# A hybrid decoder layer: the state-space products of eight heads in one block, attention by two heads, norm sums in float32r, decay products later

## The chip, the cores and the metric

One NeuronCore of a Trainium2 chip runs the kernel; the other cores are idle. The metric is device time in microseconds of one execution. Five engines work side by side, each on its own list of instructions: TensorE (matrix products and transposes, results into PSUM), VectorE, ScalarE, GpSimd (POOL) and SyncE, whose queue loads the weights. PSUM has eight banks of 128 x 512 float32; this kernel gives three to the large products (tag `pj`) and five to everything else (tag `bg`).

## The reference, cut to what matters

One layer, 256 tokens of width 1024, all float32, batch 1:

```python
h = h + 0.5 * rmsnorm(swiglu(rmsnorm(h, ...), w_gate, w_up, w_down), ...)      # width 2816
u = rmsnorm(h, mix_pre_g)
z, xbc, dt_raw, q, k, v, gate_logits = split(u @ w_in)
y_ssd = ssd_branch(z, xbc, dt_raw, ...)           # 32 heads of 64, 4 groups of 8 heads, state 128
y_att = diff_attn_branch(q, k, v, ...)            # 8 heads, two score maps each, values 128 wide
merged = gates[:, :, 0] * y_ssd + gates[:, :, 1] * y_att
h = h + rmsnorm(merged @ w_out, mix_post_g)
h = h + 0.5 * rmsnorm(swiglu(...), ...)           # a second feed-forward layer
```

The state-space branch: a causal convolution over four tokens and SiLU on x, B and C; dt = softplus(dt_raw + bias); for every head, y[t] = sum over s <= t of (C[t]·B[s]) exp(acum[t] - acum[s]) dt[s] x[s], with acum the running sum of dt times a negative number of the head; then + D x, times SiLU(z), and a norm over each group's 512 channels. The attention: for each head, softmax(map 1) - lam softmax(map 2), both causal with a linear penalty on distance, times v, and a norm over each head's 128 outputs.

## The kernel before, in words

**Products.** Weights come in chunks of 1 MB. Each chunk is split into a high part rounded to float32r (ScalarE, `L168`) and the rest (VectorE, `L169`), and three products replace one: high x high, high x low and low x high (`mm_t` `L195`, `mm_nat` `L208`). A chunk used by `mm_t` is 48 products with 256 moving columns, one used by `mm_nat` 24 products with 512. Small products (scores, decays, the state-space products, the norm sums) are in plain float32, which the trace shows as two records each; transposes show as one.

**Buffers.** Tag `k4` holds 29 tiles of 4 KB a partition (weight halves and long-lived activations), `k3` three tiles of 3 KB (the decay matrices `E` of two heads, later the scores of an attention head), `k2` seven of 2 KB. `take()` splits weights three chunks ahead of their use.

**Stages.** Feed-forward 1; v; B and C (four chunks, `L762`); x (eight); z (eight); q and k (eight); gates (eight chunks of 512 columns); the state-space branch's output product `pws` (eight); the attention branch's output product `pwd` (four); `w_out`; feed-forward 2. Before the B and C chunks stand dt's product, softplus as a polynomial on VectorE (`L693` to `L731`) and the decay products `pac` with the triangle of ones (`L733` to `L738`), whose result goes to DRAM (`acd`) and comes back spread over all partitions (`acb`).

**The background.** The state-space work, the norms and the attention are generators which stop at priced places (`yield 1.8`). After each half of the large products the code calls `back.run(us)`, which adds `us` to an account and lets the generators issue steps until the account is used up; a `BREAK` ends the run early. The prices: 3.15 a chunk in the z and q/k stages, 1.35 per 12 products in the gate stage, 1.55 in `pws` and in the first half of `pwd`. Behind the first chunk of `pwd`, `attended()` issues all that is left. In the state-space work, each pair of heads makes E and then at once its products `py` (`L813` to `L817`), where each head fills one half of the 128 columns of the array; the VectorE update of xs (`L819`) follows. Attention is a pipeline by single heads: scores of head n, transposes of head n-1, combination of head n, values of head n-1, norm of a pair every second head, transposes of the pair's result one head later.

**Order.** Up to the gate stage the order on TensorE is made by a planner from program order and its own clock of when operands are ready; from `L1063` on TensorE follows program order exactly. ScalarE and VectorE are ordered by the planner from the v stage on.

Of the kernel before, what the change touches and what calls it, by code (L numbers as in the profile page):

```python
# [14 lines left out]
F32 = mybir.dt.float32  # L15
# [9 lines left out]
P = 128  # L25
T = 256
# [4 lines left out]
H_SSD = 32  # L31
H_ATT = 8
NEG = -1e30
K4_BUFS = 29
K3_BUFS = 3
K2_BUFS = 7
RAW_BUFS = 3
AHEAD = 3
# [11 lines left out]
def tile_hybrid_layer(ctx: ExitStack, tc: tile.TileContext, x, ffn1_pre_g, ffn1_w_gate, ffn1_w_up,  # L50
# [33 lines left out]
    def bg(shape, name):  # L84
        return ps.tile(shape, F32, tag="bg", name=name, bufs=5)
# [137 lines left out]
    def act_table(name):  # L223
        f = nc.scalar.preload_act_table_set(name)
        for prev in act_since:
            tc.add_manual_dep(f.ins, prev, order, reason="activation table")
        act_since.clear()
        act_fence[0] = f.ins.name

    def act(*args, **kw):  # L230
        a = nc.scalar.activation(*args, **kw)
# [39 lines left out]
    nc.gpsimd.memset(nhalf, -0.5)  # L271
    ones = const.tile([P, P], F32, name="ones")
    nc.gpsimd.memset(ones, 1.0)

    pw = bg([P, P], "warm")

# [416 lines left out]
    ptd = bg([P, 2, H_SSD], "ptd")  # L693
    for b in range(2):
        nc.tensor.transpose(ptd[:, b, :], dtT[:, b * P:(b + 1) * P], ident[:H_SSD, :H_SSD])
    shp = [P, 2, H_SSD]
    dx = const.tile(shp, F32, name="dx")
    nc.vector.tensor_tensor(dx, ptd, dtb.unsqueeze(1).to_broadcast(shp), ALU.add)
    e = const.tile(shp, F32, name="dte")
    w2 = const.tile(shp, F32, name="dtw2")  # L700
    pol = const.tile(shp, F32, name="dtp")
    dt = const.tile(shp, F32, name="dt")

    act_table(EXP_LN)

    lp = const.tile([P, 2, 64], F32, name="lp")
    lvv = lv.rearrange("p (a b) d -> p a b d", b=2)
    tc.keep_in_program_order(nc.vector.tensor_tensor(lp, lvv[:, :, 0, :], lvv[:, :, 1, :], ALU.mult))
    ld = const.tile([P, 2], F32, name="ld")
    nc.vector.tensor_reduce(ld, lp, AX.X, ALU.add)  # L710
    act(ld, ld, AF.Exp)
    nlam = const.tile([P, 1], F32, name="nlam")
    nc.vector.tensor_sub(nlam, ld[:, 1:2], ld[:, 0:1])
    nc.vector.tensor_scalar(nlam, nlam, -0.2, None, ALU.add)
    act(aexp, aexp, AF.Exp)

    nc.scalar.activation(e, dx, AF.Abs)
    act(e, e, AF.Exp, scale=-1.0)
    act_table(SILU)
    nc.vector.tensor_scalar(w2, e, 2.0, None, ALU.add)  # L720
    nc.vector.reciprocal(w2, w2)
    nc.vector.tensor_tensor(e, e, w2, ALU.mult)
    nc.vector.tensor_tensor(w2, e, e, ALU.mult)
    nc.vector.tensor_scalar(pol, w2, 1.0 / 17, None, ALU.mult)
    for n in (15, 13, 11, 9, 7, 5, 3):
        nc.vector.scalar_tensor_tensor(pol, pol, 1.0 / n, w2, ALU.add, ALU.mult)
    nc.vector.scalar_tensor_tensor(pol, pol, 1.0, e, ALU.add, ALU.mult)
    nc.vector.tensor_scalar(dx, dx, 0.0, None, ALU.max)
    nc.vector.scalar_tensor_tensor(dt, pol, 2.0, dx, ALU.mult, ALU.add)
    av = const.tile(shp, F32, name="av")  # L730
    nc.vector.scalar_tensor_tensor(av, dt, -1.0, aexp.unsqueeze(1).to_broadcast(shp), ALU.mult, ALU.mult)  # L731

    pac = bg([P, 512], "pac")  # L733
    for b in range(2):
        nc.tensor.matmul(pac[:H_SSD, b * P:(b + 1) * P], av[:, b, :], tri, start=True, stop=True)
    nc.tensor.matmul(pac[:, 256:288], tri, av[:, 0, :], start=True, stop=True)
    nc.tensor.matmul(pac[:, 288:320], tri, av[:, 1, :], start=True, stop=True)
    nc.tensor.matmul(pac[:, 320:352], after_m, av[:, 0, :], start=True, stop=True)  # L738
    acT = k2([H_SSD, T], "acT")
    nc.scalar.activation(acT, pac[:H_SSD, :T], AF.Copy, scale=-1.0)  # L740
    acs = const.tile([P, 3, H_SSD], F32, name="acs")
    nc.scalar.copy(acs, pac[:, 256:352].rearrange("p (a h) -> p a h", a=3))
    acd = dram.tile([H_SSD, T], F32, name="acd")
    nc.gpsimd.dma_start(acd, acT)


    cw = lambda k, c: cols_b[:, k * 24 + c:k * 24 + c + 1]

# [35 lines left out]
    def ssd_work(groups):  # L784
        for g in groups:
            X = k4([P, 2, 512], f"X{g}")
            for b in range(2):
                px = bg([P, 4, P], f"px{g}{b}")
                for c in range(4):
                    nc.tensor.transpose(px[:, c, :], xs[g][:, c, b * P:(b + 1) * P], ident)  # L790
                nc.vector.tensor_tensor(
                    X[:, b, :].rearrange("p (e q) -> p e q", q=64),
                    px.rearrange("p c (e q) -> p (c e) q", q=64),
                    dt[:, b, g * 8:(g + 1) * 8].unsqueeze(2).to_broadcast([P, 8, 64]), ALU.mult)
                yield 0.6
            for hf in range(2):
                acb = k4([P, 4, T], f"acb{g}{hf}")
                r0 = g * 8 + hf * 4
                nc.gpsimd.dma_start(acb, acd[r0:r0 + 4, :].partition_broadcast(P))
                py = bg([P, 2, T], f"py{g}{hf}")  # L800
                for pr in range(2):
                    E = k3([P, 2, 3 * P], f"E{g}{hf}{pr}")
                    for i in range(2):
                        hd = r0 + pr * 2 + i
                        lh = pr * 2 + i
                        act(E[:, i, :P], acb[:, lh, P:], AF.Relu, bias=acs[:, 1, hd:hd + 1])
                        nc.vector.tensor_scalar(E[:, i, P:T], acb[:, lh, :P], acs[:, 0, hd:hd + 1], 0.0,
                                                ALU.add, ALU.max)
                        act(E[:, i, T:], acb[:, lh, P:], AF.Exp, bias=acs[:, 2, hd:hd + 1], scale=-1.0)
                    act(E[:, :, :T], E[:, :, :T], AF.Exp, scale=-1.0)  # L810
                    nc.vector.tensor_tensor(E, E, cbm[g].unsqueeze(1).to_broadcast([P, 2, 3 * P]), ALU.mult)
                    c = hf * 2 + pr
                    for i in range(2):  # L813
                        xc = slice(c * P + i * 64, c * P + (i + 1) * 64)
                        os = slice(i * 64, (i + 1) * 64)
                        nc.tensor.matmul(py[os, pr, :], X[:, 0, xc], E[:, i, P:], start=True, stop=False)
                        nc.tensor.matmul(py[os, pr, P:], X[:, 1, xc], E[:, i, :P], start=False, stop=True)  # L817
                    dc = 96 + g * 4 + c
                    nc.vector.scalar_tensor_tensor(xs[g][:, c, :], xs[g][:, c, :], cols_b[:, dc:dc + 1],  # L819
                                                   py[:, pr, :], ALU.mult, ALU.add)  # L820
                    yield 1.8

    def ssd_norm(groups):

        def one(g):
# [3 lines left out]
            yield 1.2  # L829
            nc.vector.tensor_tensor(sq[:, 0:2, :], sq[:, 0:2, :], sq[:, 2:4, :], ALU.add)  # L830
            nc.vector.tensor_tensor(sq[:, 0, :], sq[:, 0, :], sq[:, 1, :], ALU.add)
            yield 1.1
            yield BREAK
            pn = bg([P, T], f"pn{g}")
            nc.tensor.matmul(pn, ones, sq[:, 0, :], start=True, stop=True)
# [133 lines left out]
    def att_work():  # L969


        pairs = [Pair(hp) for hp in range(4)]
        heads = [Head(hd, pairs[hd // 2]) for hd in range(H_ATT)]
        for n in range(H_ATT + 2):
            if n < H_ATT:
                heads[n].scores()
                yield 2.3
            if 0 < n <= H_ATT:
                heads[n - 1].turn()
                if n % 2 == 1 and opens:  # L980
                    opens.pop()()
            if n < H_ATT:
                heads[n].combine()
                yield 1.3
            yield BREAK
            if 0 < n <= H_ATT:
                heads[n - 1].values()
                if n % 2 == 0:
                    pairs[n // 2 - 1].norm()
                    yield 1.8  # L990
                    if n == H_ATT:
                        yield BREAK
            if n >= 3 and n % 2 == 1:
                pairs[(n - 3) // 2].turn()
                yield 0.8

    class Background:

# [190 lines left out]
```

## Time and profile before

| what | value |
|---|---|
| median of 3 runs | 746.06 us (745.94 to 746.64) |
| profiled execution | 746.09 us, of it 744.4 us span |
| TensorE busy | 734.7 us, 99% |
| VectorE, ScalarE, POOL busy | 67%, 56%, 5% |
| granted TensorE clock | 0.999 |
| DMA | 138.03 MB, mean 185 GB/s |
| B/C and x stages, about | 218 to 289 us |
| z stage, q/k stage | 289 to 345, 345 to 398 us |
| gates, `pws` | 398 to 451, 451 to 505 us |
| `pwd`, `w_out` | 505 to 548 us |

Starts in the timeline are microseconds from the span's start. The busy length of a product in the trace is longer than the distance to the next start, since products overlap in the array; the distance between starts is what a product costs. A row of the timeline merges consecutive instructions of one line (`x4`) and shows the first start.

### The profile page before, as it was taken

What the parts mean: (1) busy time and instruction counts of PE and PEld (TensorE: products, weight loads), DVE (VectorE), ACT (ScalarE), POOL (GpSimd) and SP (SyncE); (2) the same over time, 40 slices, a digit from 0 to 9 for tenths busy, and PEclk for the clock granted to TensorE, in tenths of its full rate; (3) what the DMA queues carried; (4) which work ended last, traced back from release to release, by engine and by line L of the source; (5) the groups of instructions that cost most, each with busy time, mean ns of one, the idle gap of its engine ahead of it and who ended that gap; (6) DMA issues with size and microseconds to landing.
All of it is one profiled execution on the core that took longest, in us unless ns stands there. A gap on an engine that the chain in (4) does not pass through costs nothing.

```text
span 744.4 us, 12073 instructions
## 1 busy us (share of the span) xinstructions
PE 734.7 (99%) x4953; PEld 662.5 (89%) x4953; DVE 495.6 (67%) x720; ACT 415.4 (56%) x665; POOL 40.2 (5%) x74
## 2 busy tenths in 40 slices
PE   8999999999999999999999999999999999999996
PEld 7899999888889999899998778888878999999885
DVE  6675445754677988868778987794875744664612
ACT  7554435643566566868857655881654633555512
POOL 7400000000200000000000000000020000000000
PEclk9999999999999999999999999999999999999999
DMA  9695567677253638474655545384460867644601
GB/s 320 153 316 171 186 226 255 219 234 227 64 170 116 220 124 280 145 249 147 187 181 199 198 124 175 116 280 182 164 212 20 259 194 228 224 187 158 252 0 57
DMA packets 94215, 138.03 MB, mean 185 GB/s; under 512 B 2684, under 2 KB 68304, under 8 KB 94160
## 3 DMA queue, kind: packets, MB, share of 16 engines
q1 hardware_dynamic: 91488, 129.51, 52.7%
q0 software_dynamic: 2368, 7.22, 3.1%
q8 instruction: 39, 0.64, 0.4%
q10 hardware_dynamic: 304, 0.53, 0.2%
q14 instruction: 16, 0.13, 0.1%
HBM read 136.17 MB, written 1.08 MB: 184 GB/s over the span
## 4 chain that ended last, share of the span: by engine, by line
PE 94%; DVE 2%; DMA 1%; ACT 1%; POOL 1%; issue 0%; SPq 0%; DVEq 0%; ACTq 0%; POOLq 0%
PE acc_f L433 16%; PE pgt L217 6%; PE pws L217 6%; PE pn_f L217 6%; PE pg_f L202 4%; PE pg_f L203 4%; PE pup_f L202 4%; PE pup_f L203 4%; PE pup_f L205 4%; PE pg_f L205 4%; PE pn_mx L217 3%; PE pwd L217 3%; PE pxs L202 2%; PE pxs L203 2%; PE pxs L205 2%; PE pz L205 2%
## 5 line engine op out<-in xcount | busy, mean ns | idle before, releaser
L169 DVE TENSOR_TENSOR wlo<-raw,whi 128x1024 fp32r<-128x1024 f32 (+1 forms) x246 | 289.8, 1212 | 64.1 <-ACT whi L168 61.4
L168 ACT CAST whi<-raw 128x1024 fp32r<-128x1024 f32 (+1 forms) x246 | 244.7, 1043 | 65.8 <-PE acc_f L433 27.1
L202 PE MATMUL pg_f<-u_f,whi 128*128 128x256 f32 x288 | 68.3, 279 | 0.0
L203 PE MATMUL pg_f<-u_f,whi 128*128 128x256 f32 x288 | 68.3, 279 | 0.0
L203 PE MATMUL pup_f<-u_f,whi 128*128 128x256 f32 x288 | 68.3, 279 | 0.0
L202 PE MATMUL pup_f<-u_f,whi 128*128 128x256 f32 x288 | 68.3, 279 | 0.0
L433 PE MATMUL acc_f<-whi,gh_f 128*128 128x512 f32 x176 | 58.4, 391 | 0.0
L433 PE MATMUL acc_f<-whi,gl_f 128*128 128x512 f32 x176 | 58.1, 389 | 0.0
L433 PE MATMUL acc_f<-wlo,gh_f 128*128 128x512 f32 x176 | 58.1, 389 | 0.0
L202 PEld LDWEIGHTS pg_f<-u_f,whi 128*128 128x128 f32 x288 | 54.3, 189 | 0.1
L203 PEld LDWEIGHTS pg_f<-u_f,whi 128*128 128x128 f32 x288 | 54.3, 188 | 0.1
L202 PEld LDWEIGHTS pup_f<-u_f,whi 128*128 128x128 f32 x288 | 54.3, 188 | 0.0
L203 PEld LDWEIGHTS pup_f<-u_f,whi 128*128 128x128 f32 x288 | 54.3, 188 | 0.0
L561 DVE TENSOR_TENSOR sg_f<-pup_f,sg_f 128x512 f32<-128x512 f32 x18 | 12.4, 688 | 60.8 <-PE pup_f L205 60.8
L433 PEld LDWEIGHTS acc_f<-wlo,gh_f 128*128 128x128 f32 x176 | 33.0, 188 | 6.9
L205 PE MATMUL pg_f<-u_f,wlo 128*128 128x256 f32 x288 | 39.1, 279 | 0.0
L205 PE MATMUL pup_f<-u_f,wlo 128*128 128x256 f32 x288 | 39.1, 279 | 0.0
L433 PEld LDWEIGHTS acc_f<-whi,gl_f 128*128 128x128 f32 x176 | 33.0, 188 | 6.8
L433 PEld LDWEIGHTS acc_f<-whi,gh_f 128*128 128x128 f32 x176 | 32.9, 188 | 6.7
L192 ACT CAST gh_f<-sg_f 128x512 fp32r<-128x512 f32 x18 | 11.2, 622 | 47.2 <-DVE sg_f L561 47.2
L205 PEld LDWEIGHTS pup_f<-u_f,wlo 128*128 128x128 f32 x288 | 35.9, 189 | 0.0
L205 PEld LDWEIGHTS pg_f<-u_f,wlo 128*128 128x128 f32 x288 | 35.9, 189 | 0.0
(315 smaller groups left out, 1471.9 us busy)
## 6 DMA issues: line engine op xcount, KB each, us to landing
raw<-in_w_in_dram SPq DMA_DIRECT2D x40, 1024.0 KB, 5.4
raw<-in_ffn_w_down_dram SPq DMA_DIRECT2D x22, 1024.0 KB, 5.3
raw<-in_ffn_w_gate_dram SPq DMA_DIRECT2D x20, 1024.0 KB, 6.1
raw<-in_ffn_w_up_dram SPq DMA_DIRECT2D x20, 1024.0 KB, 5.6
raw<-in_ssd_w_branch_dram SPq DMA_DIRECT2D x8, 1024.0 KB, 5.1
acb<-acd POOLq DMA_DIRECT2D x8, 512.0 KB, 5.2
raw<-in_da_w_branch_dram SPq DMA_DIRECT2D x4, 1024.0 KB, 5.3
raw<-in_w_out_dram SPq DMA_DIRECT2D x4, 1024.0 KB, 5.1
```

What stands on the lines that cost most here:

```text
L168: nc.scalar.copy(hi[:, js, :], r[:, q * nj + j:q * nj + j + n, :])
L169: nc.vector.tensor_sub(lo[:, js, :], r[:, q * nj + j:q * nj + j + n, :], hi[:, js, :].bitcast(F32))
L192: nc.scalar.copy(hi, src)
L202: nc.tensor.matmul(acc[m], wh(j)[:, cs], ah(k0 + j), start=first and j == ks[0], stop=False)
L203: nc.tensor.matmul(acc[m], wh(j)[:, cs], al(k0 + j), start=False, stop=False)
L205: i = nc.tensor.matmul(acc[m], wl(j)[:, cs], ah(k0 + j), start=False, stop=last and j == ks[-1])
L217: nc.tensor.matmul(acc, a(k0 + j), b(j), start=first and i == 0, stop=last and i == 11)
L433: nc.tensor.matmul(acc[b][q], x_[:, ts], w_(kt)[:, halves[q]], start=i == 0 and kt == 0 and x_ is ah and w_ is wh, stop=i == n - 1 and kt ...
L561: nc.vector.tensor_tensor(sg, pu_, sg, ALU.mult)
```

## The change

Six edits.

- `ssd_work`: both `acb` loads of a group are issued first, then the four E tiles of its eight heads, each a step of 1.6; then all products of the group into two PSUM tiles, and the four updates of xs, as one step of 1.6.
- `att_work`: scores, transposes, combinations and values go by two heads at a time, with doubled prices; the last pair's transposes stand in a step of their own behind a BREAK.
- `ssd_norm`: the sums of squares are split into a high and a low float32r part, and two float32r products with ones replace one float32 product. The step's price is 1.7 for 1.1.
- The softplus part becomes `dt_steps()`, called behind the first B/C chunk's products, the decay products become `decay_steps()`, called behind the third's.
- `k4` has 28 tiles for 29, `k3` five for three.
- A float32r copy of the ones is made at the start on GpSimd.

```diff
-K4_BUFS = 29
-K3_BUFS = 3
+K4_BUFS = 28
+K3_BUFS = 5
...
+    ones_r = const.tile([P, P], F32R, name="ones_r")
+    nc.gpsimd.tensor_copy(ones_r, ones)
...
+    def dt_steps():
...
+        return dt, av, nlam
+
+    def decay_steps():
+        pac = bg([P, 512], "pac")
...
+        nc.gpsimd.dma_start(acd, acT)
+        return acs, acd
...
         mm_t(acc, take(), act_u)
+        if i == 0:
+            dt, av, nlam = dt_steps()
+        if i == 2:
+            acs, acd = decay_steps()
...
+            acbs = []
             for hf in range(2):
                 acb = k4([P, 4, T], f"acb{g}{hf}")
                 r0 = g * 8 + hf * 4
                 nc.gpsimd.dma_start(acb, acd[r0:r0 + 4, :].partition_broadcast(P))
-                py = bg([P, 2, T], f"py{g}{hf}")
-                for pr in range(2):
-                    E = k3([P, 2, 3 * P], f"E{g}{hf}{pr}")
...
-                    yield 1.8
+                acbs.append(acb)
+            Es = []
+            for c in range(4):
+                acb = acbs[c // 2]
+                E = k3([P, 2, 3 * P], f"E{g}{c}")
...
+                Es.append(E)
+                yield 1.6
+            pys = [bg([P, 2, T], f"py{g}{hf}") for hf in range(2)]
+            for c in range(4):
+                py, pr, E = pys[c // 2], c % 2, Es[c]
+                for i in range(2):
+                    xc = slice(c * P + i * 64, c * P + (i + 1) * 64)
+                    os = slice(i * 64, (i + 1) * 64)
+                    nc.tensor.matmul(py[os, pr, :], X[:, 0, xc], E[:, i, P:], start=True, stop=False)
+                    nc.tensor.matmul(py[os, pr, P:], X[:, 1, xc], E[:, i, :P], start=False, stop=True)
+            for c in range(4):
+                dc = 96 + g * 4 + c
+                nc.vector.scalar_tensor_tensor(xs[g][:, c, :], xs[g][:, c, :], cols_b[:, dc:dc + 1],
+                                               pys[c // 2][:, c % 2, :], ALU.mult, ALU.add)
+            yield 1.6
...
-            yield 1.1
+            sums = k2([P, 2, T], f"sums{g}", F32R)
+            split(sums[:, 0, :], sums[:, 1, :], sq[:, 0, :])
+            yield 1.7
             yield BREAK
             pn = bg([P, T], f"pn{g}")
-            nc.tensor.matmul(pn, ones, sq[:, 0, :], start=True, stop=True)
+            nc.tensor.matmul(pn, ones_r, sums[:, 0, :], start=True, stop=False)
+            nc.tensor.matmul(pn, ones_r, sums[:, 1, :], start=False, stop=True)
...
-        for n in range(H_ATT + 2):
...
+        two = lambda n: heads[2 * n:2 * n + 2]
+        for n in range(5):
+            if n < 4:
+                for hd in two(n):
+                    hd.scores()
+                yield 4.6
+            if n > 0:
+                for hd in two(n - 1):
+                    hd.turn()
+                if opens:
                     opens.pop()()
+            if n < 4:
+                for hd in two(n):
+                    hd.combine()
+                yield 2.6
             yield BREAK
+            if n > 0:
+                for hd in two(n - 1):
+                    hd.values()
+                pairs[n - 1].norm()
+                yield 1.8
+                if n == 4:
+                    yield BREAK
+            if n > 1:
+                pairs[n - 2].turn()
                 yield 0.8
+        yield BREAK
+        pairs[3].turn()
+        yield 0.8
```

More of the change, by code (lines that the diff above doesn't have):

```diff
@@ L692, in tile_hybrid_layer @@
     nc.scalar.copy(dtT, pdt)
[L693 to L743, printed above, removed]
@@ new lines, in decay_steps @@
+    def decay_steps():
+        pac = bg([P, 512], "pac")
+        for b in range(2):
+            nc.tensor.matmul(pac[:H_SSD, b * P:(b + 1) * P], av[:, b, :], tri, start=True, stop=True)
+        nc.tensor.matmul(pac[:, 256:288], tri, av[:, 0, :], start=True, stop=True)
+        nc.tensor.matmul(pac[:, 288:320], tri, av[:, 1, :], start=True, stop=True)
+        nc.tensor.matmul(pac[:, 320:352], after_m, av[:, 0, :], start=True, stop=True)
+        acT = k2([H_SSD, T], "acT")
+        nc.scalar.activation(acT, pac[:H_SSD, :T], AF.Copy, scale=-1.0)
+        acs = const.tile([P, 3, H_SSD], F32, name="acs")
+        nc.scalar.copy(acs, pac[:, 256:352].rearrange("p (a h) -> p a h", a=3))
+        acd = dram.tile([H_SSD, T], F32, name="acd")
+        nc.gpsimd.dma_start(acd, acT)
+        return acs, acd
@@ L799, in ssd_work @@
                 nc.gpsimd.dma_start(acb, acd[r0:r0 + 4, :].partition_broadcast(P))
-                py = bg([P, 2, T], f"py{g}{hf}")
-                for pr in range(2):
-                    E = k3([P, 2, 3 * P], f"E{g}{hf}{pr}")
[L803 to L820, printed above, removed]
-                    yield 1.8
@@ new lines, in ssd_work @@
+                acbs.append(acb)
[4 more added lines that the diff above has]
+                for i in range(2):
+                    hd = g * 8 + c * 2 + i
+                    lh = c % 2 * 2 + i
+                    act(E[:, i, :P], acb[:, lh, P:], AF.Relu, bias=acs[:, 1, hd:hd + 1])
+                    nc.vector.tensor_scalar(E[:, i, P:T], acb[:, lh, :P], acs[:, 0, hd:hd + 1], 0.0,
+                                            ALU.add, ALU.max)
+                    act(E[:, i, T:], acb[:, lh, P:], AF.Exp, bias=acs[:, 2, hd:hd + 1], scale=-1.0)
+                act(E[:, :, :T], E[:, :, :T], AF.Exp, scale=-1.0)
+                nc.vector.tensor_tensor(E, E, cbm[g].unsqueeze(1).to_broadcast([P, 2, 3 * P]), ALU.mult)
+                Es.append(E)
+                yield 1.6
@@ new lines, in ssd_work @@
+            pys = [bg([P, 2, T], f"py{g}{hf}") for hf in range(2)]
+            for c in range(4):
+                py, pr, E = pys[c // 2], c % 2, Es[c]
+                for i in range(2):
+                    xc = slice(c * P + i * 64, c * P + (i + 1) * 64)
+                    os = slice(i * 64, (i + 1) * 64)
+                    nc.tensor.matmul(py[os, pr, :], X[:, 0, xc], E[:, i, P:], start=True, stop=False)
+                    nc.tensor.matmul(py[os, pr, P:], X[:, 1, xc], E[:, i, :P], start=False, stop=True)
```

55 lines of the change are left out of this document (36 added, 19 removed).

## The prediction

> **What bounds the kernel now.** I read the page first, then what TensorE waited for, then the order of time on TensorE wherever the change touches it.
>
> ```profile
> span 744.4 us, 12073 instructions
> ...
> PE 734.7 (99%) x4953; PEld 662.5 (89%) x4953; DVE 495.6 (67%) x720; ACT 415.4 (56%) x665; POOL 40.2 (5%) x74
> ```
>
> ```profile
> PE py L816 <- DVE E L811: 0.6, 1, 0.6
> PE pn_f L217 <- ACT whi L168: 0.4, 1, 0.4
> ```
>
> TensorE is never idle for long, so time leaves this kernel only if TensorE is given less to do, or loses less between kinds of work. A busy row does not show the second. The timeline of TensorE does, read from one start to the next. Here is one pair of heads' products in the stream of float32r products (128x256 moving):
>
> ```profile
> 307.44 0.28 PE L203 MATMUL pz<-u_mx,whi 128*128 128x256 f32 x1
> 307.65 0.66 PE L816 MATMUL py<-E,X 128*64 128x256 f32 x4
> 308.14 0.40 PE L817 MATMUL py<-E,X 128*64 128x128 f32 x4
> 308.46 0.39 PE L202 MATMUL pz<-u_mx,whi 128*128 128x256 f32 x1
> 308.68 0.28 PE L203 MATMUL pz<-u_mx,whi 128*128 128x256 f32 x1
> ...
> 309.27 1.07 PE L205 MATMUL pz<-u_mx,wlo 128*128 128x256 f32 x8
> 310.18 1.04 PE L790 MATMUL px<-ident,xs 128*128 128x128 f32 x8
> 310.97 0.37 PE L202 MATMUL pz<-u_mx,whi 128*128 128x256 f32 x1
> 311.17 0.28 PE L203 MATMUL pz<-u_mx,whi 128*128 128x256 f32 x1
> ```
>
> In the steady stream one product takes 0.91/8 = 0.114 us. The last one before py takes 0.21, the first one after it 0.22: 0.10 and 0.11 lost at the two edges. The block takes 0.81, in all 1.02 us. The work in it is less. A pass over 128 columns takes 0.79/8 = 0.099 (the px transposes), so about 0.20 over 256; the two heads run side by side, two records each: 2 x 0.20 + 2 x 0.10 = 0.60, up to 0.65 if passes run at the 0.11 of the stream. So 0.36 to 0.42 of each 1.02 is paid for interrupting, not for multiplying.
>
> **The change, part by part.**
>
> *Eight heads' products together.* The same 16 pairs' products, in blocks of four pairs. Each merge saves one interruption; I take the lower 0.36. Full merging is 12 merges, 4.3 us. But TensorE's order in this stage is made by the planner, which takes the earliest instruction in program order that is ready by its own clock. One E is 1.27 + 0.61 us of ScalarE:
>
> ```profile
> 300.85 1.27 ACT L231 ACTIVATE E<-acb,acs 128x128 f32<-128x128 f32 x4
> 302.02 0.61 ACT L231 ACTIVATE E<-E 128x512 f32<-128x512 f32 x1
> ```
>
> Four are 7.5 us, and with the weight casts of the meantime about twice that; between the call that issues the first two and the one that issues the products lie two chunks of 48 products, 10.9 us, and the Es themselves don't wait for TensorE. So most groups should be whole when TensorE comes to them, the first hardly. I take 10 merges: -3.6; the ends are 0 and -4.3. The two acb loads now leave POOL's queue back to back, so the second asks for its buffer earlier; behind it on POOL stands only the load of the gate biases, not read before the gate stage. The E tiles get five buffers for three, which four live Es need.
>
> The Trainium skill (TensorEngine Tiling, Key Properties) says that changing the tiling mode, not just the tile, drains TensorE. py is 128*64 and the stream 128*128, so by that rule all of the edge goes with each merge; but the first product after the px transposes, which stay 128*128, also takes 0.20 (310.97 to the next start at 311.17), so the rule is not the whole edge. By the rule alone the sum would be the same within 0.5 us.
>
> *Attention by two heads.* One head's scores, in the gate stage with 128x512 products:
>
> ```profile
> 418.81 0.85 PE L217 MATMUL pgt<-whi,u_mx 128*128 128x512 f32 x3
> 419.60 0.50 PE L883 MATMUL psc<-k,q 64*128 64x128 f32 x4
> ...
> 420.46 1.19 PE L217 MATMUL pgt<-whi,u_mx 128*128 128x512 f32 x4
> 421.49 1.08 PE L217 MATMUL pgt<-wlo,u_mx 128*128 128x512 f32 x4
> 422.41 1.08 PE L217 MATMUL pgt<-whi,u_mx 128*128 128x512 f32 x4
> ```
>
> Four products take 0.92, one 0.23. Before psc 0.79 for three (+0.10), the block 0.86, after it 1.03 for four (+0.11): 1.07, with 0.65 of work as in py. Four merges save 4 x 0.42 = -1.7; the ends are -0.8 (only the edges) and -1.7. Two heads need four of the five PSUM banks for a moment; VectorE empties them in order, and the next user of a bank comes a step of 12 products (3 x 0.92 = 2.75 us) later. The transposes of the probabilities and the value products are 128*128 like the stream, and the transposes px above cost their own passes and one late product; two such blocks side by side save at most that 0.09, eight times, which I leave out.
>
> *Norm sums in float32r.*
>
> ```profile
> 404.25 0.60 PE L835 MATMUL pn<-sqy,ones 128*128 128x256 f32 x2
> 404.49 1.28 PE L217 MATMUL pgt<-whi,u_mx 128*128 128x512 f32 x4
> 405.61 1.08 PE L217 MATMUL pgt<-wlo,u_mx 128*128 128x512 f32 x4
> ```
>
> The block takes 0.24 and the four products behind it 1.12 for 0.92: 0.44 for one sum. Two float32r products of 256 columns take 0.23 by the stream: 4 x 0.21 = -0.85. The split costs a ScalarE copy and a VectorE subtraction of 128x256, four times, under half a microsecond each by the neighbouring row; a background step lies between them and the product, so 2.75 us of TensorE work covers them. Uncovered, it would be about 1 us a group.
>
> ```profile
> L831 DVE TENSOR_TENSOR sqy<-sqy x4: 418/425/427, 369.6 to 397.9; 128x256 f32<-128x256 f32 x4
> ```
>
> The POOL copy for ones_r falls into POOL's idle 4.29 us at the start, while the input is on its way:
>
> ```profile
> 5.96 0.73 POOL L322 TENSOR_SCALAR r_f<-ss_f 128x1 f32<-128x1 f32 x1 [4.29 <-ACT sq_f L317]
> ```
>
> *Decay products behind the third chunk.*
>
> ```profile
> 223.90 0.52 PE L205 MATMUL pbc<-u_mx,wlo 128*128 128x256 f32 x3
> 224.75 0.62 PE L735 MATMUL pac<-m,av 128*32 128x128 f32 x4 [0.33 <-DVE av L731]
> ```
>
> Three products take 0.85 for 0.34: 0.5 us, of which an edge of 0.1 stays. Saved: 0.4. The chain on VectorE that makes av now starts after the first chunk, some 5 us later, with the convolution of that chunk behind it on VectorE. Its PSUM buffer is wanted by the fourth chunk about 13 us later. I cost this at nothing; if the cover fails, the fourth chunk waits at most those 5 us. The decay table then reaches DRAM some 10 us later, near 240, and the E above, the second to read it, runs at 300.85.
>
> *The end of attention.* The background's steps carry prices, and each run of it buys so many. The state-space groups go from 1.2 + 4 x 1.8 = 8.4 to 9.2 units, the norms from 5.2 to 5.8: 5.6 units more. The 16 runs of 3.15 up to the gates buy 50.4, and what is left goes from 4.0 to 9.6. At 1.35 a step that is four steps of 2.75 us. Working through all the runs by hand, the first scores come out behind the eighth gate step instead of the third, and the last value products (heads 6 and 7) behind the first step of the attention branch's product, where today the last transpose stands before it. Then only one step and the third pair's transposes (2.75 + 0.35 = 3.1 us) cover the last pair's norm. That chain today:
>
> ```profile
> 499.25 0.39 PE L927 MATMUL po<-v,aT 128*128 128x128 f32 x2
> ```
>
> ```profile
> 499.68 0.60 ACT L939 ACTIVATE o<-po 128x512 f32<-128x512 f32 x1
> ...
> 505.63 0.68 ACT L964 ACTIVATE o<-pto,g 128x512 fp32r<-128x512 f32 x1
> ```
>
> ```profile
> 501.00 0.68 DVE L941 TENSOR_REDUCE ro<-o 128x4 f32<-128x512 f32 x1
> ...
> 503.41 0.68 DVE L946 TENSOR_TENSOR o<-po,ro 128x512 f32<-128x512 f32 x1
> ```
>
> From po's last start to the end of L946 it is 504.09 - 499.25 = 4.8 us, with weight casts between; bare, 0.60 + 0.68 + 0.68 = 1.96, and a few short steps and hand-overs. So TensorE waits 0 to 1.7 beyond the 3.1, and then 0.3 to 0.5 for the 0.68 copy of the last transposes, which the next products read. I take +1.0; the ends are 0.3 and 2.2.
>
> *One weight buffer less* (28 for 29). The tightest place is the first gate chunk:
>
> ```profile
> 394.87 2.35 DVE L169 TENSOR_TENSOR wlo<-raw,whi 128x1024 fp32r<-128x1024 f32 x2
> ```
>
> ```profile
> 398.29 1.08 PE L217 MATMUL pgt<-whi,u_mx 128*128 128x512 f32 x4
> 399.20 1.08 PE L217 MATMUL pgt<-wlo,u_mx 128*128 128x512 f32 x4
> ```
>
> Its low halves are ready at 397.22 and read from 399.20 on: 2 us to spare. With one buffer less, and the norms' buffers freed about three steps later, I take +0.3; the ends are 0 and 3.
>
> **The sum**: -3.6 - 1.7 - 0.85 - 0.4 + 1.0 + 0.3 = -5.25. The profiled execution took 746.09 (its span 744.4 and 1.7 around it), the median of the runs is 746.06. Forecast **740.9**.
>
> **The rivals.**
>
> 1. *The products scatter.* The planner finds the Es ready one by one and places them as today. For it: today py stands between two products of one chunk (L203 and L202, above), so the planner does take what is ready. Against: the Es no longer wait for products in between. Then only 1.7 + 0.85 + 0.4 go, less 1.3 of new waits: 744.4, and 745.5 with the upper ends of the tail.
>
> 2. *TensorE starves at the gates* (slower). The splits of the gate chunks wait for buffers that the late norms hold. It decides once a chunk's low halves come more than the 2 us later; with a buffer freed only at the end of a chunk, the loss goes in steps of up to 2.75 us on each of some four chunks: +11 less the 5.25 gained, 751 or so. Against: the norms free three buffers for every two that they take. For it: 28 buffers and the norms' delay meet just there. By the Trainium skill (TensorE: Matmul & The Clock Gate, Part 1) an idle window of about 3.4 us also halves the clock for a while; no run here shows such a gap after the start.
>
> 3. *The second feed-forward layer changes pace.* Its products run slower than the first's, with the same instructions:
>
> ```profile
> 35.14 0.91 PE pg_f L205 x8
> ```
>
> ```profile
> 578.00 0.94 PE pg_f L205 x8
> ```
>
> 864 products at 0.03 per eight are 3.2 us. The slow pace sets in at the start of the stage and holds; what sets it, this profile doesn't show. If another arrival flips it, 740.9 - 3.2 = 737.7; the first layer, reached as before, could flip the other way only by the shifted addresses.
>
> **How the numbers follow.** Forecast (739.5 to 743) 0.58, scattered products 0.16, starved or otherwise late 0.13, second layer at the fast pace 0.13. The measurement tells 0.2% from no change, that is 744.57 and 747.55. Forecast and pace are faster, half of the scattered case too, and a quarter of an incomplete starvation: 0.58 + 0.13 + 0.08 = 0.79, less a little for what I have not thought of: 0.77. Within: 0.08 and part of the third: 0.13. Slower: 0.10. The range leaves out the full starvation and half of the flip: 737.2 to 746.
>
> **What would show it.** Right: blocks of 16 py records of each line with one pair of 0.1 edges, 2.6 to 2.8 us long; psc blocks of 8 and 8; no records of L835's kind taking 0.24; no wait at pac; a wait of about 1 us at the last pto or the products behind it; the first scores near 416 instead of 407.5. Wrong: py in blocks of 4; TensorE waiting for wlo or whi in the gate stage; any other pace in stages that the change leaves alone.

## The result and the profile after

| | before | after |
|---|---|---|
| median of five runs, us | 746.06 (742.68 to 746.64) | 739.55 (739.38 to 739.94) |
| profiled execution, us | 746.09 | 739.55 |
| its span, us | 744.4 | 737.8 |

The ratio of the two kernels is 0.9921. Its 95% interval, 0.9899 to 0.9944, lies below 1, so the kernel is faster, by 0.8%; between the profiled executions it is 6.5 us. One run of the kernel before took 742.68; the last section says what that probably is. Among the experiments two executions stand far outside the others of their kernel, 753.34 us (products behind each pair) and 1490.46 us (the kernel before with one product), and no argument rests on them.

From the page of the kernel after:

```profile
PE 728.3 (99%) x4953; PEld 663.0 (90%) x4953; DVE 493.0 (67%) x724; ACT 415.1 (56%) x669; POOL 38.7 (5%) x75
```

TensorE is still busy for 99% of the span and issues as many instructions as before (4953), yet its busy time fell from 734.7 to 728.3. That is what fewer interruptions look like: the same records, closer together. Its waits after the start (us in total, times, longest):

```profile
PE pn_f L217 <- ACT whi L168: 0.8, 1, 0.8
PE pu_f L334 <- POOL un_f L367: 0.5, 1, 0.5
PE pwd L217 <- ACT o L985: 0.4, 1, 0.4
```

The wait of py for E (0.6) and that of pac for av (0.3) are gone, no wait for a weight half has come in the gate stage, and one new wait stands at the last transposes of attention (0.4).

**Where the time went.** Each line below is a group of like products: behind the colon stand the shortest, middle and longest duration in ns, then the first and the last start. The first start of a stage's products tells when the stage begins. Kernel before, then kernel after; the B and C products, in the same view, start at 218.7 and 219.1:

```profile
L202 PE MATMUL pz<-u_mx,whi x128: 275/277/386, 289.2 to 345.5; 128*128 128x256 f32 x128
...
L217 PE MATMUL pgt<-whi,u_mx x128: 387/394/585, 398.3 to 449.6; 128*128 128x512 f32 x128
...
L433 PE MATMUL acc_mx<-whi,mh x32: 389/389/477, 528.2 to 551.7; 128*128 128x512 f32 x32
```

```profile
L202 PE MATMUL pz<-u_mx,whi x128: 275/277/367, 289.3 to 340.3; 128*128 128x256 f32 x128
...
L217 PE MATMUL pgt<-whi,u_mx x128: 387/392/505, 393.4 to 441.3; 128*128 128x512 f32 x128
...
L435 PE MATMUL acc_mx<-whi,mh x32: 389/389/477, 522.3 to 545.2; 128*128 128x512 f32 x32
```

| stretch | before | after | difference |
|---|---|---|---|
| start to B and C | 218.7 | 219.1 | +0.4 |
| B and C, x | 70.5 | 70.2 | -0.3 |
| z, q and k | 109.1 | 104.1 | -5.0 |
| gates, `pws`, `pwd` | 129.9 | 128.9 | -1.0 |
| `w_out` to the end | 216.2 | 215.5 | -0.7 |

Five of 6.5 us come from the stretch with the state-space products.

**The state-space block.** TensorE's timeline in the kernel after, one group of eight heads:

```profile
305.63 1.07 PE L205 MATMUL pz<-u_mx,wlo 128*128 128x256 f32 x8
306.62 0.66 PE L833 MATMUL py<-E,X 128*64 128x256 f32 x4
...
307.33 0.65 PE L833 MATMUL py<-E,X 128*64 128x256 f32 x4
...
307.98 0.65 PE L833 MATMUL py<-E,X 128*64 128x256 f32 x4
...
309.43 0.66 PE L800 MATMUL px<-ident,xs 128*128 128x128 f32 x4
```

A pair inside the block takes 0.65 (307.33 to 307.98), where a pair alone took 0.81 and 0.21 more at its edges. The last pair takes 0.80, from 308.63 to the next group's px transposes, which follow directly here. Three of the four groups are whole like this; the last is split, three pairs and one, with a single product of the stream between them. That makes 11 merges of the 12 possible.

**The scores of two heads**, with the gate stage's products around them:

```profile
414.94 1.08 PE L217 MATMUL pgt<-whi,u_mx 128*128 128x512 f32 x4
415.95 0.50 PE L904 MATMUL psc<-k,q 64*128 64x128 f32 x4
...
416.71 0.49 PE L904 MATMUL psc<-k,q 64*128 64x128 f32 x4
...
417.56 1.20 PE L217 MATMUL pgt<-whi,u_mx 128*128 128x512 f32 x4
418.60 1.08 PE L217 MATMUL pgt<-wlo,u_mx 128*128 128x512 f32 x4
```

Two heads take 1.61 (415.95 to 417.56), and 0.10 and 0.13 at the edges (1.01 and 1.04 for four products of 0.91): 1.84, against 2 x 1.07. A merge saves 0.30. The other three blocks of scores take 1.61 or 1.62 too.

**A norm sum**, **the end of attention** and **the transposes of h in the `w_out` stage**, kernel after:

```profile
387.67 0.28 PE L855 MATMUL pn<-sums,ones_r 128*128 128x256 f32 x1
...
387.91 0.28 PE L202 MATMUL pk<-u_mx,whi 128*128 128x256 f32 x1
...
503.26 1.04 PE L973 MATMUL pto<-ident,o 128*128 128x128 f32 x8
504.73 1.31 PE L217 MATMUL pwd<-whi,o 128*128 128x512 f32 x4 [0.43 <-ACT o L985]
505.88 1.08 PE L217 MATMUL pwd<-wlo,o 128*128 128x512 f32 x4
...
540.70 0.39 PE L435 MATMUL acc_mx<-wlo,mh 128*128 128x512 f32 x1
540.93 1.04 PE L334 MATMUL pu_f<-ident,h 128*128 128x128 f32 x8
541.72 0.48 PE L435 MATMUL acc_mx<-whi,mh 128*128 128x512 f32 x1
```

The sum's two float32r products run in step with the stream: 0.24, and nothing is late behind them. The last transposes take 1.47 to the next product (eight transposes alone are 0.79), and the four products behind take 1.15 for 0.91: 0.9 us in all. The same transposes of h in the kernel before:

```profile
546.60 0.39 PE L433 MATMUL acc_mx<-wlo,mh 128*128 128x512 f32 x1
547.23 1.23 PE L332 MATMUL pu_f<-ident,h 128*128 128x128 f32 x8 [0.25 <-DVE h L412]
548.22 0.47 PE L433 MATMUL acc_mx<-whi,mh 128*128 128x512 f32 x1
```

From the product ahead to the product behind they take 1.62 before and 1.02 after: 0.6 us that no edit aimed at.

### The profile page after: what moved, and what is told of

Same layout as the page of the kernel before. It is cut to its first block, busy times and chain, and to the rows that moved or that the text cites. A ratio compares the mean times of both kernels' runs of the same rounds, so it can differ in the third digit from the quotient of the medians.

```text
span 737.8 us, 12094 instructions
## 1 busy us (share of the span) xinstructions
PE 728.3 (99%) x4953; PEld 663.0 (90%) x4953; DVE 493.0 (67%) x724; ACT 415.1 (56%) x669; POOL 38.7 (5%) x75
## 4 chain that ended last, share of the span: by engine, by line
PE 97%; POOL 1%; DMA 1%; ACT 0%; issue 0%; DVE 0%; SPq 0%; DVEq 0%; POOLq 0%
PE acc_f L435 16%; PE pgt L217 6%; PE pws L217 6%; PE pn_f L217 6%; PE pg_f L203 5%; PE pg_f L202 5%; PE pup_f L202 5%; PE pup_f L203 5%; PE pup_f L205 5%; PE pg_f L205 5%; PE pn_mx L217 3%; PE acc_mx L435 3%; PE pwd L217 3%; PE pxs L202 2%; PE pxs L203 2%; PE pz L202 2%
```

## The experiments

Unless said otherwise each kernel is the changed one with the edit shown. Times are medians; the ratio is to the kernel before.

| kernel | us | ratio (95%) |
|---|---|---|
| the change | 739.55 | 0.9921 (0.9899 to 0.9944) |
| products behind each pair | 744.99 | 1.0001 (0.9980 to 1.0023) |
| single heads in attention | 740.26 | 0.9929 (0.9913 to 0.9944) |
| norm sums in float32 | 740.65 | 0.9938 (0.9917 to 0.9959) |
| decay products early | 740.17 | 0.9931 (0.9909 to 0.9953) |
| 27 weight buffers | 739.94 | 0.9924 (0.9904 to 0.9944) |
| before, with the block alone | 742.06 | 0.9957 (0.9940 to 0.9973) |
| larger steps in `pws` | 743.35 | 0.9973 (0.9955 to 0.9991) |
| larger steps, scores apart | 739.67 | 0.9924 (0.9907 to 0.9941) |
| four products in feed-forward 2 | 737.52 | 0.9894 (0.9875 to 0.9912) |
| one product in feed-forward 2 | 736.40 | 0.9877 (0.9857 to 0.9896) |
| before, with that one product | 743.19 | 0.9963 (0.9951 to 0.9976) |
| four products in feed-forward 1 | 740.81 | 0.9936 (0.9911 to 0.9960) |

### Products behind each pair again

```diff
             for c in range(4):
+                if c % 2 == 0:
+                    py = bg([P, 2, T], f"py{g}{c // 2}")
                 E = k3([P, 2, 3 * P], f"E{g}{c}")
...
-                Es.append(E)
-                yield 1.6
-            pys = [bg([P, 2, T], f"py{g}{hf}") for hf in range(2)]
-            for c in range(4):
-                py, pr, E = pys[c // 2], c % 2, Es[c]
                 for i in range(2):
...
-            yield 1.6
+                yield 2.0
```

> The changed kernel with one thing undone: the products of each pair of heads stand behind that pair's E again (steps of 2.0, so that a group costs the background the same 9.2 units). If each interruption of the float32r stream costs 0.34 us, as the two edges and the inside of a block of the profiles give it, some 11 or 12 blocks more make the z and q/k stages 3.7 to 4.1 us longer than the 104.05 us of the changed kernel (before: 109.13), about 743.4 in all with the second feed-forward layer at its slow pace. If the stage got shorter through the wait for E that went (0.75 us before the first block) and through the planner's new order instead, the blocks come back and the stage stays at 104 to 105.

It took 744.99, 5.4 more than the change. Waits and timeline of this kernel:

```profile
PE py L830 <- DVE E L826: 0.6, 1, 0.6
```

```profile
306.64 0.28 PE L202 MATMUL pz<-u_mx,whi 128*128 128x256 f32 x1
306.85 0.66 PE L830 MATMUL py<-E,X 128*64 128x256 f32 x4
...
307.66 0.39 PE L203 MATMUL pz<-u_mx,whi 128*128 128x256 f32 x1
307.88 0.28 PE L202 MATMUL pz<-u_mx,whi 128*128 128x256 f32 x1
```

The blocks of eight records, their edges and the wait for E are back. The z, q and k stages take 108.9 us for 104.1, that is 4.8 more: 0.6 of it is the wait, and 4.2 over 11 merges are 0.38 each. The rest of the 5.4 is 0.5 at the end of attention. The expectation of 743.4 was too low: it priced a block at 0.34, and had neither the wait for E nor the end of attention in its sum. What the merging saves is the interruption, since the records and their order within a pair are the same.

### The block alone, on the kernel before

The `ssd_work` of the change and its buffers, and nothing else of it:

```diff
-K4_BUFS = 29
-K3_BUFS = 3
+K4_BUFS = 28
+K3_BUFS = 5
...
+            acbs = []
+            Es = []
...
+                Es.append(E)
+                yield 1.6
+            pys = [bg([P, 2, T], f"py{g}{hf}") for hf in range(2)]
...
```

> The kernel before with only the products of eight heads gathered (and the buffers 28 and five that they need): single heads in attention, float32 sums, decay products early. If most of the gain is this one edit, the stages from the first z product to the first gate product, 109.13 before and 104.05 in the changed kernel, take 104.4 to 104.6 (two float32 sums lie in them), and the whole is 741 to 741.5, less what a late end of attention costs at pwd (up to 2). If the edits need each other, the stage stays above 106.

742.06, 4.0 less than before. The groups of its stages:

```profile
L202 PE MATMUL pz<-u_mx,whi x128: 275/276/368, 289.7 to 340.8; 128*128 128x256 f32 x128
...
L217 PE MATMUL pgt<-whi,u_mx x128: 388/392/585, 394.2 to 445.0; 128*128 128x512 f32 x128
```

The z, q and k stages take 104.5 us for the kernel before's 109.1. So 4.6 of the stage's 5.0 come with this edit alone, and the two float32r sums that lie there make up the rest. With the edits undone singly in the next runs the medians add up to 4.0 + 0.7 (two heads) + 1.1 (sums) + 0.6 (decay) = 6.4, of 6.5 measured. That is closer than the terms are: stage by stage the sums give 0.8 and the decay products 0.3. Between executions the start alone differs by more than that: the products of the first feed-forward layer set in anywhere between 33.15 and 34.56 us in the profiled executions, though the code up to there is nearly the same in all of these kernels.

### The edits of small size, each undone

Norm sums in float32:

```diff
-            sums = k2([P, 2, T], f"sums{g}", F32R)
-            split(sums[:, 0, :], sums[:, 1, :], sq[:, 0, :])
...
-            nc.tensor.matmul(pn, ones_r, sums[:, 0, :], start=True, stop=False)
-            nc.tensor.matmul(pn, ones_r, sums[:, 1, :], start=False, stop=True)
+            nc.tensor.matmul(pn, ones, sq[:, 0, :], start=True, stop=True)
```

> The changed kernel with the norm sums as one float32 product again, without the split. If a float32 product pays for its passes, each of the four sums costs 0.44 again instead of 0.23: +0.8 us, 740.4. If what the sums cost is an edge that any foreign product pays, little changes: under +0.2.

740.65, 1.1 more than the change. In the profiled execution 0.45 of its 1.25 lies ahead of the first feed-forward layer's products, where the two kernels do the same; the 0.8 left is four sums at 0.2.

Decay products early:

```diff
+    dt, av, nlam = dt_steps()
+    acs, acd = decay_steps()
     bT = k4([P, 4, T], "bT")
...
-        if i == 0:
-            dt, av, nlam = dt_steps()
-        if i == 2:
-            acs, acd = decay_steps()
```

> The changed kernel with the softplus chain and the decay products ahead of the B and C chunks again. If moving them took away TensorE's wait for av, that wait (0.3 to 0.5 us) is back and the time is 740.0; the stage from the first B/C product to the first x product, 23.78 us in the changed kernel and 24.33 before, is 24.3 again. If the wait went for another reason, the stage stays at 23.8.

740.17, 0.6 more. The wait for av at pac (0.3 us) is back where it was, and the stage of B and C takes 24.3 us again for 23.8. But the x stage behind it takes 46.2 for 46.4, so over both stages the later decay products save 0.3.

Single heads in attention (with the larger steps, since single heads have other prices):

```diff
-SSD_US = 1.55
+SSD_US = 1.9
...
-        for n in range(5):
-            if n < 4:
-                for hd in two(n):
-                    hd.scores()
-                yield 4.6
+        for n in range(H_ATT + 2):
+            if n < H_ATT:
+                heads[n].scores()
+                yield 2.3
...
```

> The changed kernel with attention by single heads as before, and 1.9 units of background per step of the state-space branch's product, so that by the account attention ends ahead of the attention branch's product. If a merge of two heads' scores is worth the 0.32 us that the profiles give (1.81 us for a block of two with its edges, 2 x 1.07 for two single ones), the four merges are lost, +1.3 us, and the late end's 0.9 us is won back: 739.9 to 740.0, and no wait at pwd. If gathering the heads is worth more than its blocks, because VectorE and ScalarE work in longer pieces, it is 741 or more; if it is worth nothing, 738.7.

740.26, 0.7 more, with no wait at the last transposes. Four merges of 0.30 save 1.2, and the later end of attention costs 0.9, which would leave 0.3. The stages from the gates to `pwd` differ by 0.5 in the profiled executions, the medians by 0.7; where the rest comes from is not traced, and since the step is larger as well, this run does not undo the attention edit alone. About half of what is saved at the scores is left at the end.

One weight buffer less again:

```diff
-K4_BUFS = 28
+K4_BUFS = 27
```

> The changed kernel with one more weight buffer taken away (27). If the buffer that the change gave up costs nothing, one more costs nothing either: 739.6 (739.3 to 740.0) and no new wait of TensorE for weights. If weights arrive just in time in the gate stage, 740.5 or more, with waits for split weights at the gates.

739.94, 0.4 more, and no new wait of TensorE for weights. The gate stage takes 48.7 us in both kernels, so the 2 us that its first weight halves have to spare are enough. The 0.4 lies elsewhere: the scores of the last two heads take 2.03 us for 1.62, and the wait at the last transposes is 0.1 longer.

### A longer step in `pws`, so that attention ends earlier

```diff
-SSD_US = 1.55
+SSD_US = 1.9
```

> The changed kernel with 1.9 instead of 1.55 units of background for each 12 products of the state-space branch's output product. By the account of the steps the last transposes of attention then come out two steps before the attention branch's product, as before the change. If the late end of attention cost what the profile of the changed kernel shows there (about 0.6 us before the last transposes, 0.4 us before the products that read them), the time is 738.6 and TensorE waits for nothing at pwd. If the denser background starves something in exchange, the time is 739.5 or more and a new wait stands in the stage of pws.

743.35, 3.8 more. The wait at the last transposes is gone, but the scores of heads 6 and 7 now come directly behind the value products and transposes of the pair before, at 469.81. TensorE's timeline there:

```profile
470.79 0.59 PE L905 MATMUL psc<-k,q 64*128 64x256 f32 x2
473.47 0.49 PE L904 MATMUL psc<-k,q 64*128 64x128 f32 x2 [2.09 <-DVE ol L986]
...
474.66 2.07 PE L217 MATMUL pws<-whi,yh 128*128 128x512 f32 x4
476.53 1.47 PE L217 MATMUL pws<-wlo,yh 128*128 128x512 f32 x4
477.83 1.07 PE L217 MATMUL pws<-whi,yl 128*128 128x512 f32 x4
```

The second head's scores wait 2.09 us for VectorE, and the first four products behind take 1.87 (474.66 to 476.53) and the next four 1.30 for the usual 0.91. The view by windows, whose column `PEclk` (third from the right) is the granted clock, says why:

```profile
471.40:473.40 2.00, 0.00 (x0) 0.00 (x0) 2.00 (x4) 1.32 (x2) 0.00 (x0) 1.00 0.19 12
...
473.60:474.60 1.00, 1.00 (x4) 0.41 (x4) 1.00 (x3) 0.33 (x2) 0.00 (x0) 0.66 0.60 188
474.60:475.50 0.90, 0.90 (x3) 0.75 (x3) 0.90 (x2) 0.00 (x0) 0.00 (x0) 0.50 1.04 405
...
477.00:477.50 0.50, 0.50 (x3) 0.42 (x2) 0.50 (x1) 0.50 (x3) 0.00 (x0) 0.67 0.00 0
```

During the wait the granted clock is still 1.00; about half a microsecond after work resumes it falls to 0.50 and stays there for 3.4 us (by the shares of the windows at either end, from 473.9 to 477.3). The halved clock costs 0.96 and 0.39 on those eight products. The block of scores (469.81 to 474.66) takes 4.85 us for 1.61; that is 3.2 more, of it 2.1 the wait. Less the 0.9 that the earlier end of attention gives back, this makes 3.7 of the 3.8 measured. The Trainium skill (TensorE: Matmul & The Clock Gate, Part 1) has the clock halved after at least one idle window of about 3.4 us; here 2.1 us of idleness are enough, so the measurement sets the bound lower for this execution. Not every execution pays for the clock: in 4 of the 12 the mean granted clock is 0.999 and the time 740.9 to 742.0, in the other 8 it is 0.993 to 0.997 and the time 743.1 to 745.5. Whether the wait is shorter in those four, or meets the clock at another moment, is not known, since only one execution, at 0.997, was profiled. The new waits at the end of attention in the change (0.43) leave the clock at 1.00.

To keep the longer step without that wait, a BREAK was put ahead of the scores of the third and the fourth pair:

```diff
-SSD_US = 1.55
+SSD_US = 1.9
...
+            if n in (1, 2):
+                yield BREAK
```

> As the run with 1.9 units per step, with a break ahead of the scores of the third and fourth pair of heads, so that they come a step of 12 products behind the value products and the transposes. If TensorE waited there for PSUM banks (four for the scores, one each for values and transposes, five in all), the wait of 2.1 us and the slow products behind it are gone, attention still ends ahead of pwd, and the time is 738.6 to 738.8. If the denser background itself is too much for VectorE and ScalarE, another wait of a microsecond or more shows up in pws and the time stays above 740.

739.67: the clock stays up and the wait at the last transposes is gone, but the block of scores still takes 2.57 us for 1.61, and the two nearly cancel. In both kernels the second head's last scores start just after `ol` (`L986`), with which VectorE empties the bank of the transposes, late because weight splits come first. So the scores seem to wait for the transposes' bank, the fourth one that they want, and twelve products more between make the block 1.0 us longer instead of 3.2. Neither theory had that.

### What sets the pace of the second feed-forward layer

Four more products of 128 by 128, in float32, between its chunks, whose result nobody reads:

```diff
             split(gh[:, o:o + 2, :], gl[:, o:o + 2, :], sg)
+            if tag == "f2" and j in (3, 5, 7, 9):
+                t = nc.tensor.matmul(bg([P, P], f"pulse{j}"), ident, ident, start=True, stop=True)
+                tc.add_manual_dep(t.ins, done_up.ins.name, order, reason="behind gate and up")
```

> The changed kernel with one float32 product of ones of the identity, 128x128, behind the fourth, sixth, eighth and tenth pair of weight chunks of the second feed-forward layer; nobody reads its result. Each costs about 0.4 us with its edges. If the pace of the float32r stream (0.113 or 0.118 us for 256 columns) is a state that an interruption draws anew and that then holds, some of the stretches between the pulses run at 0.113 throughout and others at 0.118, and each stretch of 96 products at the fast pace gives back 0.45 us. If the pace belongs to the stage (addresses, other traffic), all stretches keep 0.118 and the time is 741.1.

737.52: TensorE is given more to do, and the kernel is 2.0 us faster. In its trace eight products take 0.94 or 0.95 up to the first of the four, and 0.90 or 0.91 behind it to the end of the stage; the other three change nothing. So the pace was not drawn anew at each. Then one product alone, behind the first gate and up chunks (`j == 2`):

> The changed kernel with one 128 by 128 float32 product more, behind the first gate and up chunks of the second feed-forward. If an interruption sets the pace and the pace is then held, the 768 products of the eight chunk pairs behind it run at 0.1135 us in place of 0.118: 768 x 0.0045 = 3.5 less, 0.3 to 0.4 for the interruption, so 736.4 (736.0 to 737.0). If the place of the interruption matters and this one sets the slower pace again: 739.9.

736.40, the fastest of all these kernels: 3.15 less than the change, ratio 0.9877 to the kernel before. Its timeline, from the slow pace through the one product:

```profile
571.20 1.10 PE L205 MATMUL pg_f<-u_f,wlo 128*128 128x256 f32 x8
572.14 0.28 PE L202 MATMUL pg_f<-u_f,whi 128*128 128x256 f32 x1
...
580.62 0.38 PE L566 MATMUL pulse<-ident 128*128 128x128 f32 x2
580.76 0.36 PE L202 MATMUL pg_f<-u_f,whi 128*128 128x256 f32 x1
...
582.68 1.07 PE L205 MATMUL pg_f<-u_f,wlo 128*128 128x256 f32 x8
583.59 0.28 PE L202 MATMUL pg_f<-u_f,whi 128*128 128x256 f32 x1
```

Eight products take 0.94 ahead of it and 0.91 behind. The pace then holds for the rest of the stage, which the groups show by the median of a product (the middle one of the three durations) and by the start of the stage that follows. The change, then the kernel with the one product:

```profile
L202 PE MATMUL pg_f<-u_f,whi x144: 280/282/282, 569.4 to 664.4; 128*128 128x256 f32 x144
...
L435 PE MATMUL acc_f<-whi,gh_f x88: 388/389/477, 671.6 to 730.8; 128*128 128x512 f32 x88
```

```profile
L202 PE MATMUL pg_f<-u_f,whi x144: 276/276/365, 569.3 to 661.3; 128*128 128x256 f32 x144
...
L435 PE MATMUL acc_f<-whi,gh_f x88: 389/389/476, 668.3 to 727.5; 128*128 128x512 f32 x88
```

282 against 276 ns; the stage takes 99.0 us for 102.2. In these two kernels the pace turns at the product itself. The same product in the kernel before:

> The kernel before with that one product. If the pace of the second feed-forward and the change are independent of each other, this saves 3.1 as there: 743.0 where the kernel before runs at 746.1, and the change is worth 6.5 by the kernel with the one product on either side. If the faster executions of the kernel before (742) were something else than this pace, some runs here lie near 739.

743.19, 2.9 less than the kernel before, and the change is worth 6.8 us with it, 6.5 without: to 0.3 us the pace and the change are independent. But the trace of this run does not show the product at work:

```profile
578.39 1.07 PE L205 MATMUL pg_f<-u_f,wlo 128*128 128x256 f32 x8
579.30 0.28 PE L202 MATMUL pg_f<-u_f,whi 128*128 128x256 f32 x1
...
587.47 0.38 PE L564 MATMUL pulse<-ident 128*128 128x128 f32 x2
```

Eight products take 0.91 already 9 us ahead of it, and so from the start of the stage (576.57). In this execution the layer set in at the faster pace ahead of the only edit, and what brought it there is not known.

The same four products in the first feed-forward layer, where the pace is the faster one from the start:

> The changed kernel with four such products in the first feed-forward, where the pace is 0.113 already, and none in the second. If an interruption of this kind always sets 0.113: four interruptions of 0.3, 739.6 + 1.2 = 740.8, the products behind them at 0.113. If it turns the pace over, the stretches behind the first and the third run at 0.118: 384 x 0.0045 = 1.7 more, 742.5.

740.81, as the first theory had it: the pace behind them stays at 276 ns, and the four interruptions lengthen the stage of gate and up by 1.0, 0.25 each (the median is 1.3 higher). In the feed-forward layers such a product was followed by the faster pace in all of its ten places in four kernels. In two of them the pace was slow ahead and turned there; in the other eight it was the faster one already, and the product did not turn it back.

## Why the prediction was right

The forecast was 740.9 and the result 739.55, inside the range. The gain is 1.3 us larger than forecast, and two waits of 0.6 that stood in no term, for E and at the transposes of h, account for nearly all of it. The other misses, up to 0.5 each, cancel, which is luck. By terms:

| term | forecast | measured | from |
|---|---|---|---|
| state-space blocks | -3.6 (10 merges at 0.36) | -4.1 (11 at 0.37) | z, q and k: -5.0, less the next row and two sums |
| wait of py for E | not in the sum | -0.6 | waits before and after |
| scores by two heads | -1.7 (4 at 0.42) | -1.2 (4 at 0.30) | 1.84 for two heads |
| norm sums | -0.85 | -0.8 | 0.24 each, nothing late behind |
| wait at pac | -0.4 | -0.3 | B and C stage -0.5, x stage +0.2 |
| end of attention | +1.0 | +0.9 | last transposes and the products behind |
| one buffer less | +0.3 | 0 | no wait for weights; not undone alone |
| transposes of h | not in the sum | -0.6 | 1.62 to 1.02 |
| elsewhere | 0 | +0.5 | ahead of feed-forward 1 |
| sum | -5.25 | -6.2 | -6.5 in all; 0.3, from the gates to `pwd`, not traced |

**The state-space blocks** were argued from rows of a single pair. The lower end of what is lost, 0.36, was the right one, since a pair inside the block takes 0.65. The count of 10 was one short, and the group held to be the hardest, the first, is whole; the last one is split. The step that failed is a row the prediction quoted and did not use: the 0.6 us that py waited for E. When products of four pairs stand behind all four Es, that wait has no place left, and it should have been a term of its own.

**The scores** are the mis-sized term. The prediction put 0.65 of work into a block of 0.86, "as in py". But the block of two heads takes 1.61, twice a head's block within 0.1: psc's own products need nearly all of its 0.86, and a merge saves little but the edges. The lower end of the bounds was -0.8, and -1.2 lies between; a py pair, with another tile and other widths, was not the nearest row for psc's inside.

**The norm sums, the wait at pac and the end of attention** came out as worked out, to 0.1: no late product behind a sum, no wait at pac, first scores at 415.95 where 416 was forecast, and one wait at the last transposes, 0.43 with 0.5 more around it.

**The weight buffer** was not given back alone, so its price of 0 is read from the waits only; one buffer less again costs 0.4, and not at the weights. +0.3 was a hedge without a row.

**What was not foreseen** is the 0.6 at the transposes of h. Their product waited for VectorE's residual sum before and doesn't after. In the kernel with the block alone the `w_out` stage is shorter by 0.6 too, and in the kernel with the products behind each pair, so neither attention nor the merging is needed for it. What those two share with the change are the buffer counts, the two acb loads one behind the other and the dearer steps of the state-space work; which of them does it was not tried. The 0.5 at the start lies ahead of all edits but the copy of ones, and is not the change's: the kernel before with the one product, where nothing else is changed, starts its first layer 0.6 later than the kernel before (33.74 for 33.15).

**The rivals.** Scattered products were priced at 744.4 to 745.5, and the kernel that scatters them takes 744.99: right in price, and not what happened, as E no longer waits for products. Starvation at the gates did not come, and with a buffer less still doesn't. The changed pace did not come with the change (282 ns in the second layer, as before), but its price was right: the forecast of 3.2 us less is 3.15 when one product sets it. Its condition, "if another arrival flips it", stays open: one product turns the pace within the stage, but in one profiled execution the layer was at the faster pace from its start, and what decides that was not found.

## What to carry to other kernels

On a TensorE that is busy 99% of the time, read the distance between starts, not busy time: a block between two streams pays for its edges and its own start, 0.37 us here for eight short products, and batching such blocks saves that much per merge while the work stays the same. Price each kind of block from its own rows, and list every wait that the new order leaves without a place, not only the ones that the edit aims at. Batching also asks for several buffers at once, and behind a wait of 2.1 us the clock halved here: look at the granted clock in narrow windows, since the mean over the span (0.997) hides it.

## What the runs showed of the hardware

**Two paces of the same stream.** Back-to-back float32r products of 256 columns run 0.1138 or 0.1175 us apart (0.91 and 0.94 for eight), with the clock granted in full. A stream keeps its pace for hundreds of products until something interrupts it. One float32 product of 128 columns, 0.14 us and an edge of about 0.1 on one side, turned the slower pace into the faster one in both places of the second feed-forward layer where it met it, and gained 3.15 us with one product; where the pace was the faster one already, it stayed. It is not true of every interruption: behind the third group's state-space block and transposes, in the q and k stage of the change, the stream sets in at the slower pace (0.94 for eight) and holds it for 17 us. What distinguishes the two kinds of interruption was not found, and what the array does differently was not seen.

The kernel before has executions near 742 beside the many near 746 (3 of 17 at 741.5 to 742.8 in the last comparison, the others at 745.5 to 747.3). In its profiled execution the stage of gate and up takes 102.1 us in the second layer and 98.7 in the first, with the same products: 3.5 less would be 742.6. With the one product in place, 11 of 12 times lie together at 742.9 to 743.8. That the executions near 742 have the faster pace is argued, since none of them was profiled; that the layer can set in at that pace, the trace of the kernel before with the one product shows (0.91 ahead of the product).

**The clock after a short wait.** 2.1 us of waiting brought the granted clock to 0.50 for 3.4 us, half a microsecond after the work went on. By their times and mean clocks, 8 of that kernel's 12 executions met such a fall and 4 (0.999) did not. The shorter wait of the next kernel, whose block of scores took 0.96 longer, left it at 1.00.
